# A hybrid decoder block in fp32: the S5 scan in eight blocks of four state columns on VectorE, and every gate, branch output, w_out and w_up chunk computed token-major

## The chip, the core and the metric

The kernel runs on one core of one Trainium2 chip. The metric is device time in microseconds (us) of one execution, the median of several runs. TensorE (PE) multiplies, VectorE (DVE), ScalarE (ACT) and GpSimd (POOL) do elementwise work, SyncE (SP) issues most of the loads. Each engine works through its own instructions in order. A "weight load" (PEld) is TensorE taking in the stationary operand of a matmul, which every matmul here does afresh.

## The reference

One decoder layer on 256 tokens of width 2048, all in float32:

```python
xn = rms_norm(h)
u_s5, u_lru, q, k, v, gate_logits = split(xn @ w_in)      # 1024 each, gates 3 x 2048
g_s5, g_lru, g_attn = split(sigmoid(gate_logits + b_gate))
merged = g_s5 * (s5(u_s5) @ w_br_s5) + g_lru * (rglru(u_lru) @ w_br_lru) + g_attn * (attn(q, k, v) @ w_br_attn)
h = h + merged @ w_out
h = h + relu(rms_norm(h) @ w_up) ** 2 @ w_down            # hidden width 8192
out = rms_norm(h)
```

S5: 64 groups of 16 channels with 64 complex states each. Per group, the input goes through a small matrix to the states (B), each state runs a linear recurrence h[t] = lam_bar * h[t-1] + bu[t] over the 256 tokens, the states go through another small matrix (C) to 16 outputs, and then come a skip term, tanh-GELU, and a gate through w_glu. RG-LRU is a gated real recurrence, attention is stick-breaking (exp, log and a running sum by a triangular product) in 8 heads.

## The kernel before

**Weight stream.** All large products draw on one stream of 520 weight units of 256 x 512 (512 KB). A unit is loaded on SP into `raw` (three buffers, loads three units ahead), cast on ScalarE into `hi` (L134: rounded to the reduced format fp32r), and VectorE forms the rest, `lo = raw - hi` (L135). `hi` and `lo` have three buffers each and are made two units ahead. Activations are split the same way, and each product is the sum of three: hi by hi, hi by lo, lo by hi.

**Two forms of a unit.** `chunk` (L183, tile `mm_...`) is channel-major: the weights are stationary and 256 tokens move, 24 matmuls of 256 columns a unit, and the result has channels on partitions. `chunk_tok` (L203, tile `mt_...`) is token-major: 128 tokens of the activation are stationary and 512 weight columns move, 12 matmuls of 512 columns, tokens on partitions. Here 148 units are channel-major and 372 token-major. A chunk is 512 output columns: 8 units where the input is 2048 wide, 4 where it is 1024.

**Order of work.** The stages follow one another in the stream: LRU input, S5 input, gates and branch product of LRU (branch 1), q, k and v with attention, gates and product of attention (branch 2), gates of S5, w_glu, product of S5, w_out, then four quarters of the MLP, each 32 units of w_up and 32 of w_down. What is not a weight unit is a side task: a generator in `later(..., rate)`. After each unit, `pump` gives each task as many steps as its rate (1.0 is a step a unit), and the instructions of a step are placed on their engines behind that unit's. `finish` runs a task to its end at once.

**S5.** `s5_scan` (L583) is such a task at rate 1.2. It runs in 16 blocks of NT = 2 state columns (a column holds 128 of the 4096 states). In a block, `s5_tables` makes cos and sin of the turning angle (`tc`, `ts`): the angle sum on POOL, rounding on ScalarE and VectorE (L557), magnitude and two sines on ScalarE (L559 to L561), which needs ScalarE's table for sine (ACT_TABLE_LOAD). Six small DMAs on SP put the operands of the B products side by side (`stk`, two buffers). The B products `ps_v` (L600) are copied to `v` (L602). Two products and a sum a component turn the states back by the angle (L614 to L620; L614, `t4 = vr * s`, on POOL), four scans (L628) run the recurrence with the real radius `rad`, each of 256 tokens, and six more products and sums turn forward (L630 to L638; L630 on POOL). Then eight matmuls of 32 output rows, L647 and L648, form `ps_y`: a block uses two of the array's four groups of 32 columns (`tile_position`). L650 adds the skip term to `us5`. After every fourth block GELU of a pair of column tiles runs on POOL, its tanh on ScalarE.

**Gates and branches.** `gates` (L685) and `branch` (L706) do three of four column chunks token-major and chunk 3 channel-major. The products are gated on VectorE and summed on POOL into `merged`; its token-major chunks are transposed by `blocks` (L673, 32 x 32 blocks on VectorE, L677) in `split_tok` while the next units run, and split into hi and lo.

**w_out and MLP.** w_out's chunks 0 to 2 are token-major; their residual sums are transposed in the side task `residual` and split. Chunk 3 is channel-major, and `to_tokens` transposes its sum the other way, sixteen blocks ahead of the sums of the second norm (`norm2`). In each MLP quarter, chunks 0 to 2 of w_up are token-major (`hidden`: transposes, square on ScalarE into `hd_hi` and on POOL, L991 the difference `hd_lo`), and chunk 3 is channel-major and needs no transpose (L1016). w_down is token-major.

Of the kernel before, what the change touches and what calls it, by code (L numbers as in the profile page):

```python
# [14 lines left out]
P = 128  # L15
L = 256
# [7 lines left out]
NT = 2  # L24
PAR = {"norm_mix_g": 16, "norm_mlp_g": 16, "b_gate": 48, "s5_d": 8, "s5_b_glu": 8, "lru_conv_b": 8,
# [12 lines left out]
GELU_C = math.sqrt(2.0 / math.pi)  # L38

# [6 lines left out]
def hybrid_block(ctx: ExitStack, tc: tile.TileContext, io, out):  # L46
# [213 lines left out]
    stk = sp.tile([96, 2, NT, 2, L], F32R, name="stk")  # L260
# [90 lines left out]
    cco = pp.tile([P, 2, 32, 16], F32, tag="v", name="cco")  # L351
# [13 lines left out]
    def s5_params():  # L365
# [55 lines left out]
        for k, (p, q, op) in enumerate(((cb_, ib_, ALU.add), (ib_, cb_, ALU.subtract))):  # L421
            u = [pp.tile([P, 32, 16], F32, tag=f"t{2 * k + i + 1}", name=f"cq{k}_{i}") for i in range(2)]
            g.tensor_tensor(u[0], cco[:, 0], p, ALU.mult)
            yield
            g.tensor_tensor(u[1], cco[:, 1], q, ALU.mult)
            yield
            for h in range(2):
                r_ = slice(64 * h, 64 * h + 64)
                g.tensor_tensor(ce[r_, k, :, h, :], u[0][r_], u[1][r_], op)
                yield  # L430
# [45 lines left out]
    def lru_half(c, us):  # L476
        parts = []
        for m in range(2):
            src = ((lp, "xc"), (lp, "r"), (lp, "i"), (lp, "th")) if m == 0 else ((pp, "tc"), (pp, "ts"), (pp, "t2"), (pp, "t4"))
            t = [p_.tile([P, 2, L], F32, tag=n_, name=f"lru_{n_}{c}", **({"bufs": 2} if n_ in ("tc", "ts") else {})) for p_, n_ in src]  # L480
# [62 lines left out]
    S5_RATE = 1.2  # L543

    def s5_tables(b):
# [7 lines left out]
        def gen():  # L553
            nc.gpsimd.tensor_tensor(c, fhi[:, q, :].unsqueeze(3).broadcast_to(sh), flo[:, q, :].unsqueeze(2).broadcast_to(sh), ALU.add)
# [19 lines left out]

    def s5_stack(b, ts=range(NT)):
        if b >= 32 // NT:
            return
        for t in ts:
            k = (b % 2) * NT + t
            for i, w_ in enumerate((ux[:, 0:4:2, :], ux[:, 1:3, :], ux[:, 0:4:3, :])):  # L580
                nc.sync.dma_start(stk[i * 32:i * 32 + 32, b % 2, t].bitcast(F32), w_[k * 32:k * 32 + 32].bitcast(F32))

    def s5_scan():  # L583
        tabs, more = s5_tables(0)
# [4 lines left out]
        s5_stack(0)  # L589
        for _ in range(5):  # L590
            yield
        for b in range(32 // NT):
            c, s = tabs
            ct = b // 2
            v = pp.tile([P, 2, NT, L], F32, tag="v", name=f"v{b}")
            vr, vi = v[:, 0], v[:, 1]
            for t in range(NT):
                ps = pss.tile([P, CH], F32, tag="ps", name=f"ps_v{b}")
                for i in range(2):
                    nc.tensor.matmul(ps[:, i * L:(i + 1) * L], stk[:, b % 2, t, 1, i * P:(i + 1) * P], stk[:, b % 2, t, 0, :], start=i == 0, stop=True,  # L600
                                     skip_group_check=True)
                nc.scalar.copy(v[:, :, t, :], v2(ps))  # L602
            if b % 2 and ct + 1 < WT:
                s5_split(ct + 1)
            more = iter(())
            if b + 1 < 32 // NT:
                tabs, more = s5_tables(b + 1)
            next(more, None)
            yield
            t1 = pp.tile([P, NT, L], F32, tag="t1", name=f"t1_{b}")  # L610
            t2 = pp.tile([P, NT, L], F32, tag="t2", name=f"t2_{b}")
            t3 = pp.tile([P, NT, L], F32, tag="t3", name=f"t3_{b}")
            t4 = pp.tile([P, NT, L], F32, tag="t4", name=f"t4_{b}")
            nc.gpsimd.tensor_tensor(t4, vr, s, ALU.mult)  # L614
            nc.vector.tensor_tensor(t1, vr, c, ALU.mult)
            nc.vector.tensor_tensor(t2, vi, s, ALU.mult)
            yield
            nc.vector.tensor_tensor(t1, t1, t2, ALU.add)
            nc.vector.tensor_tensor(t3, vi, c, ALU.mult)
# [19 lines left out]
            for _ in range(3):  # L639
                yield  # L640
# [466 lines left out]
```

## Time and profile before

| | |
|---|---|
| median of three runs | 1566.22 us (1565.44 to 1566.68) |
| the profiled execution, own time | 1565.52 us |
| its span in the profile | 1563.8 us |
| mean granted TensorE clock | 0.992 of full speed |
| TensorE busy | 1520.8 us, 97% |
| VectorE, ScalarE, POOL busy | 1162.6, 807.9, 219.0 us |
| S5's stretch (first LRU gate to w_glu) | 113.16 to 645.64 us |
| the MLP | from 847.46 us |

Rows of groups read: line, engine, operation, output <- inputs with shape, count | busy us, mean ns of one | idle time just before them and what ended it. Rows in order of time read: start and duration in us, engine, line, operation. Rows of waits read: waiting instruction <- what released it: us in all, count, longest.

### The profile page before, as it was taken

How to read it: one execution, taken by the hardware profiler on the slowest of the kernel's cores; microseconds unless marked ns; L12 is line 12 of the kernel's file. 1: busy time of each engine (PE TensorE's matmuls, PEld its weight loads, DVE VectorE, ACT ScalarE, POOL GpSimd, SP SyncE). 2: the span in 40 equal slices, each digit the busy share in tenths (PEclk: the TensorE clock that was granted, in tenths of full speed). 3: DMA queues.
4: the chain of work that ended last, by engine and by line, in shares of the span. 5: the costliest groups of instructions: out<-in, count | busy, mean ns of one | idle time of the engine just before them, and what ended most of it. 6: DMA issues, size and time to landing. Idle time of an engine off the chain costs nothing.

```text
span 1563.8 us, 21927 instructions
## 1 busy us (share of the span) xinstructions
PE 1520.8 (97%) x8430; PEld 1316.4 (84%) x8430; DVE 1162.6 (74%) x1417; ACT 807.9 (52%) x976; POOL 219.0 (14%) x172
## 2 busy tenths in 40 slices
PE   9899999989999999999999999999999999999997
PEld 9897789978877788988889888888988898888986
DVE  5887998878979899578698895558655685558755
ACT  7468555486756555543444544344433444344443
POOL 5301113112112322101000010000100000000111
PEclk9999999999999999999999999999999999999999
DMA  9555665545536565655756556555566566655554
GB/s 282 156 169 172 188 197 174 176 135 168 178 115 199 172 188 176 205 192 167 279 191 194 183 167 197 194 193 191 189 194 196 189 190 192 196 190 192 191 196 148
DMA packets 88491, 291.78 MB, mean 187 GB/s; under 512 B 12738, under 2 KB 16962, under 8 KB 88130
## 3 DMA queue, kind: packets, MB, share of 16 engines
q1 hardware_dynamic: 87954, 287.14, 57.2%
q10 hardware_dynamic: 432, 3.24, 0.6%
q8 instruction: 66, 1.08, 0.3%
q14 instruction: 39, 0.32, 0.1%
HBM read 281.95 MB, written 2.10 MB: 182 GB/s over the span
## 4 chain that ended last, share of the span: by engine, by line
PE 80%; DVE 11%; ACT 4%; issue 3%; DMA 1%; DVEq 0%; ACTq 0%
PE mt_w_down L212 7%; PE mt_w_down L213 7%; PE mt_w_down L214 7%; PE mm_w_in L198 5%; PE mm_w_in L196 5%; PE mt_w_up L214 5%; PE mm_w_in L197 5%; PE mt_w_up L213 5%; PE mt_w_up L212 5%; DVE lo L135 4%; PE mt_w_in L213 3%; PE mt_w_in L214 3%; PE mt_w_in L212 3%; PE mm_w_up L198 2%; PE mm_w_up L197 2%
## 5 line engine op out<-in xcount | busy, mean ns | idle before, releaser
L135 DVE TENSOR_TENSOR lo<-raw,hi 128x1024 fp32r<-128x1024 f32 (+1 forms) x521 | 660.9, 1272 | 327.6 <-ACT hi L134 323.0
L134 ACT CAST hi<-raw 128x1024 fp32r<-128x1024 f32 (+1 forms) x521 | 545.3, 1049 | 661.2 <-PE mt_w_down L214 197.6
L198 PE MATMUL mm_w_in<-xhi,lo 128*128 128x256 f32 x704 | 202.1, 288 | 7.3 <-DVE lo L135 7.3
L196 PE MATMUL mm_w_in<-xhi,hi 128*128 128x256 f32 x704 | 202.4, 288 | 1.8 <-DVE rs L297 1.2
L213 PE MATMUL mt_w_down<-lo,hd_hi 128*128 128x512 f32 (+1 forms) x528 | 202.1, 383 | 0.0
L212 PE MATMUL mt_w_down<-hi,hd_hi 128*128 128x512 f32 (+1 forms) x528 | 202.1, 383 | 0.0
L214 PE MATMUL mt_w_down<-hi,hd_lo 128*128 128x512 f32 (+1 forms) x528 | 202.0, 383 | 0.0
L197 PE MATMUL mm_w_in<-xlo,hi 128*128 128x256 f32 x704 | 201.3, 286 | 0.0
L213 PE MATMUL mt_w_up<-lo,hhi 128*128 128x512 f32 x384 | 150.0, 391 | 2.5 <-DVE lo L135 2.5
L214 PE MATMUL mt_w_up<-hi,hlo 128*128 128x512 f32 x384 | 149.5, 389 | 0.0
L212 PE MATMUL mt_w_up<-hi,hhi 128*128 128x512 f32 x384 | 149.4, 389 | 0.0
L213 PE MATMUL mt_w_in<-lo,xhi 128*128 128x512 f32 x352 | 140.8, 400 | 7.5 <-DVE lo L135 7.3
L212 PE MATMUL mt_w_in<-hi,xhi 128*128 128x512 f32 x352 | 141.4, 403 | 3.9 <-ACT hi L134 3.9
L198 PEld LDWEIGHTS mm_w_in<-xhi,lo 128*128 128x128 f32 x704 | 136.9, 195 | 9.5 <-DVE lo L135 9.1
L196 PEld LDWEIGHTS mm_w_in<-xhi,hi 128*128 128x128 f32 x704 | 137.3, 195 | 4.1 <-issue 2.6
L214 PE MATMUL mt_w_in<-hi,xlo 128*128 128x512 f32 x352 | 139.4, 396 | 0.0
L197 PEld LDWEIGHTS mm_w_in<-xlo,hi 128*128 128x128 f32 x704 | 137.3, 195 | 0.2
L214 PEld LDWEIGHTS mt_w_down<-hi,hd_lo 128*128 128x128 f32 x528 | 99.2, 188 | 19.4
L212 PEld LDWEIGHTS mt_w_down<-hi,hd_hi 128*128 128x128 f32 x528 | 99.2, 188 | 19.3
L213 PEld LDWEIGHTS mt_w_down<-lo,hd_hi 128*128 128x128 f32 x528 | 99.2, 188 | 19.2
L988 POOL TENSOR_TENSOR reluT<-reluT 128x1024 f32<-128x1024 f32 x12 | 23.8, 1984 | 642.9 <-ACT hd_hi L987 519.5
L213 PEld LDWEIGHTS mt_w_up<-lo,hhi 128*128 128x128 f32 x384 | 72.1, 188 | 19.3 <-DVE lo L135 4.5
(328 smaller groups left out, 2600.0 us busy)
## 6 DMA issues: line engine op xcount, KB each, us to landing
raw<-in_w_in SPq DMA_DIRECT2D x175, 512.0 KB, 3.6
raw<-in_w_up SPq DMA_DIRECT2D x128, 512.0 KB, 3.4
raw<-in_w_down SPq DMA_DIRECT2D x128, 512.0 KB, 4.1
raw<-in_w_out SPq DMA_DIRECT2D x32, 512.0 KB, 4.3
raw<-in_w_br_lru SPq DMA_DIRECT2D x16, 512.0 KB, 3.8
raw<-in_w_br_attn SPq DMA_DIRECT2D x16, 512.0 KB, 3.5
raw<-in_w_br_s SPq DMA_DIRECT2D x16, 512.0 KB, 3.5
stk<-ux SPq DMA_DIRECT2D x96, 64.0 KB, 3.3
```

The costliest lines, as they stand in the source:

```text
L134: anchor["act"] = nc.scalar.copy(h[:, k, :], r[:, k, :]).ins
L135: anchor["dve"] = nc.vector.tensor_tensor(l_[:, k, :], r[:, k, :], h[:, k, :].bitcast(F32), ALU.subtract).ins
L196: nc.tensor.matmul(o, wh[:, kk, s], xh, start=first and ct % 2 == 0, stop=False, skip_group_check=True)
L197: nc.tensor.matmul(o, wh[:, kk, s], xl, start=False, stop=False, skip_group_check=True)
L198: mm = nc.tensor.matmul(o, wl[:, kk, s], xh, start=False, stop=last and ct % 2 == 1, skip_group_check=True)
L212: nc.tensor.matmul(banks[j], xh[:, s], wh[:, a:b], start=kt == 0, stop=False)
L213: nc.tensor.matmul(banks[j], xh[:, s], wl[:, a:b], start=False, stop=False)
L214: return nc.tensor.matmul(banks[j], xl[:, s], wh[:, a:b], start=False, stop=kt == ng * UK - 1)
L988: nc.gpsimd.tensor_tensor(rT, rT, rT, ALU.mult)
```

## The change

1. NT goes from 2 to 4, so S5 has 8 blocks of four state columns, and elementwise operations in it work on 1024 elements a partition instead of 512. All of them are on VectorE, the table's angle sum and GELU's products too; scans run onto their own input. `stk` has one buffer, and its DMAs are issued in the scan steps, three behind each of the first four scans. The rate is 1.27, with about one large VectorE operation to a step. The C products of a block are 16 matmuls over all four column groups, neighbours in different groups. GELU becomes a side task of its own with two operations on ScalarE and two on VectorE, and its factor of one half moves into w_glu's split and gate.
2. `gates` and `branch` do all four chunks token-major, as do w_out and w_up in every quarter: 76 units change from 24 matmuls of 256 columns to 12 of 512. `split_tok(3)`, `residual(3)` and `hidden` of the last chunk now run as side tasks at rate 2.0 (two groups of four transposes a unit), and the units that need their result finish them first (`ms`, `hs`, `hs_`). `to_tokens` is gone.

```diff
-NT = 2
+NT = 4
-    stk = sp.tile([96, 2, NT, 2, L], F32R, name="stk")
+    stk = sp.tile([96, NT, 2, L], F32R, name="stk")
-    S5_RATE = 1.2
+    S5_RATE = 1.27
-            nc.gpsimd.tensor_tensor(c, fhi[...], flo[...], ALU.add)
+            nc.vector.tensor_tensor(c, fhi[...], flo[...], ALU.add)
     def s5_scan():
...
+            tt(t1, vr, c, ALU.mult)
+            yield
+            tt(t2, vi, s, ALU.mult)
+            yield
+            tt(t1, t1, t2, ALU.add)
+            yield
+            tt(t3, vi, c, ALU.mult)
+            yield
+            tt(vr, vr, s, ALU.mult)
+            yield
+            tt(t3, t3, vr, ALU.subtract)
             next(more, None)
             yield
...
+            for x_ in (t1, t3):
                 for t in range(NT):
                     j = b * NT + t
+                    tt_scan(x_[:, t, :], rad[:, j:j + 1].broadcast_to([P, L]), x_[:, t, :])
+                    if b + 1 < WT and x_ is t1:
+                        s5_stack(t)
+                    yield
...
+            for k, w_ in enumerate((t2, t1)):
+                for t in range(NT):
+                    nc.tensor.matmul(ps[t * 32:t * 32 + 32, 0:L], ce[:, k, b * NT + t, :, :], w_[:, t, :], start=k == 0, stop=k == 1,
+                                     skip_group_check=True, tile_position=(0, t * 32))
...
+    def gelu(b):
+        y = us5[:, b - 1:b + 1, :]
+        nc.scalar.activation(g1, y, AF.Square)
+        nc.vector.scalar_tensor_tensor(g1, g1, 1.0 / GELU_K, y, ALU.add, ALU.mult)
+        yield
+        nc.scalar.activation(g1, g1, AF.Tanh, scale=GELU_C * GELU_K)
+        nc.vector.scalar_tensor_tensor(y, g1, 1.0, y, ALU.add, ALU.mult)
...
-        banks = (chunk_tok if c < 3 else chunk)("w_in", GATE0 + 4 * idx + c, D, xs)
+        banks = chunk_tok("w_in", GATE0 + 4 * idx + c, D, xs)
-        banks = (chunk_tok if c < 3 else chunk)(wname, c, W, ys)
+        banks = chunk_tok(wname, c, W, ys)
+    last = later([split_tok(3, mlp.tile([P, 4, L], F32, tag="reluT", name="mT3", bufs=2))], 2.0)
-        rq = later([residual(c)], 1.0)
-    banks = chunk("w_out", 3, D, ms)
+        rq = later([residual(c)], 2.0 if c == 3 else 1.0)
     def norm2():
-        yield from to_tokens()
+        while rq[0]:
+            yield
-            banks = (chunk if last else chunk_tok)("w_up", ...)
+            banks = chunk_tok("w_up", ...)
+            hq = later([hidden(r, h_[:, k, :], l_[:, k, :], f"{q}_{c}")], 2.0 if c == FQ // CH - 1 else 1.0)
         def hs_(kt):
+            if kt >= 12:
+                finish(hq)
```

How it moves instructions, at three places. A row is a line, an operation, output <- inputs with the tiles' running numbers, and the shape; lines are those of the kernel the list is of.

VectorE in a block of S5, from one `lo` of the weight stream to the next in the kernel before (`us_99` is `us5`, `t_3` are t1 to t4):

```order
L135 TENSOR_TENSOR lo_2286<-raw_2247,hi_2285 128x1024
L615 TENSOR_TENSOR t_3_2301<-v_2265,tc_2055 128x512
L616 TENSOR_TENSOR t_3_2302<-v_2265,ts_2056 128x512
L619 TENSOR_TENSOR t_3_2303<-v_2265,tc_2055 128x512
L618 TENSOR_TENSOR t_3_2301<-t_3_2301,t_3_2302 128x512
L620 TENSOR_TENSOR t_3_2303<-t_3_2303,t_3_2304 128x512
L557 SCALAR_TENSOR_TENSOR ts_2281<-ts_2281,tc_2280 128x512
L715 TENSOR_TENSOR merged<-mt_w_br_lru_0_64_2203,gate_2_0_2197 128x512
L715 TENSOR_TENSOR merged<-mt_w_br_lru_1_64_2204,gate_2_1_2200 128x512
L135 TENSOR_TENSOR lo_2323<-raw_2283,hi_2322 128x1024
```

The same place in the changed kernel, a whole backward turn (`s_v` is v, `s_t` holds t1 and t2, `t_2` is t3, L558 is the angle sum of the next table, L136 makes `lo`):

```order
L136 TENSOR_TENSOR lo_2552<-raw_2510,hi_2551 128x1024
L615 TENSOR_TENSOR s_t<-s_v,tc_2094 128x1024
L617 TENSOR_TENSOR s_t<-s_v,ts_2095 128x1024
L136 TENSOR_TENSOR lo_2584<-raw_2549,hi_2583 128x1024
L619 TENSOR_TENSOR s_t<-s_t 128x1024
L136 TENSOR_TENSOR lo_2615<-raw_2581,hi_2614 128x1024
L621 TENSOR_TENSOR t_2_2472<-s_v,tc_2094 128x1024
L136 TENSOR_TENSOR lo_2646<-raw_2612,hi_2645 128x1024
L623 TENSOR_TENSOR s_v<-s_v,ts_2095 128x1024
L558 TENSOR_TENSOR tc_2534<-fhi,flo 128x1024
L625 TENSOR_TENSOR t_2_2472<-t_2_2472,s_v 128x1024
L136 TENSOR_TENSOR lo_2679<-raw_2643,hi_2678 128x1024
```

Eight operations of 512 elements stood between two `lo`; now at most three of 1024 stand there, and the turn is spread over five units. L623, before on POOL, is among them.

ScalarE in the first attention of the kernel before (L752 to L755 are a head's logits, their magnitude, exp and log; L559 to L561 the sines of a table):

```order
L752 COPY z_3391<-ps_z_3393 128x384
L559 ACTIVATE tc_3298<-ts_3299 128x512
L753 ACTIVATE s_3392<-z_3391 128x384
L560 ACT_TABLE_LOAD
L560 ACTIVATE ts_3299<-ts_3299 128x512
L754 ACT_TABLE_LOAD
L754 ACTIVATE s_3392<-s_3392 128x384
L561 ACT_TABLE_LOAD
L561 ACTIVATE tc_3298<-tc_3298,half_pi 128x512
L755 ACT_TABLE_LOAD
L755 ACTIVATE s_3392<-s_3392 128x384
```

ScalarE at the same place of the changed kernel (L743 to L746 are the head, L572 and L576 the split of the next block's operands, L607 copies B products):

```order
L761 ACT_TABLE_LOAD
L135 CAST hi_3153<-raw_3114 128x1024
L607 COPY s_v<-ps_v_3132 128x2x256
L607 COPY s_v<-ps_v_3136 128x2x256
L743 COPY z_3140<-ps_z_3142 128x384
L572 CAST ux<-us_99 128x256
L744 ACTIVATE s_3141<-z_3140 128x384
L576 ACTIVATE ux<-bco,par 128x2x64
L745 ACTIVATE s_3141<-s_3141 128x384
L576 ACTIVATE ux<-bco,par 128x2x64
L746 ACTIVATE s_3141<-s_3141 128x384
```

A head and a table's sines no longer alternate, and one table load stands ahead of the head instead of four in it. Over the whole program the list has 50 table loads before and 31 after.

VectorE from the last transposes of a quarter's third w_up chunk on, before (L991 and L1016 make `hd_lo`, L1016 that of the last chunk):

```order
L677 STREAM_TRANSPOSE reluT_2_8653<-relu_2_8618 32x2x4x32 x4
L135 TENSOR_TENSOR lo_8763<-raw_8726,hi_8762 128x1024
L135 TENSOR_TENSOR lo_8795<-raw_8760,hi_8794 128x1024
L135 TENSOR_TENSOR lo_8825<-raw_8792,hi_8824 128x1024
L991 TENSOR_TENSOR hd_lo_2_8617<-reluT_2_8653,hd_hi_2_8616 128x1024
L135 TENSOR_TENSOR lo_8856<-raw_8822,hi_8855 128x1024
L1016 TENSOR_TENSOR hd_lo_2_8617<-relu_3_0_8883,hd_hi_2_8616 128x512
L135 TENSOR_TENSOR lo_8898<-raw_8853,hi_8897 128x1024
L1016 TENSOR_TENSOR hd_lo_2_8617<-relu_3_1_8888,hd_hi_2_8616 128x512
L135 TENSOR_TENSOR lo_8916<-raw_8895,hi_8915 128x1024
```

And from the third chunk's `hd_lo` (L974) on in the changed kernel:

```order
L974 TENSOR_TENSOR hd_lo_2_7844<-reluT_2_7868,hd_hi_2_7843 128x1024
L136 TENSOR_TENSOR lo_7999<-raw_7977,hi_7998 128x1024
L136 TENSOR_TENSOR lo_8022<-raw_7996,hi_8021 128x1024
L683 STREAM_TRANSPOSE reluT_3_8037<-relu_3_8014 32x2x4x32 x8
L136 TENSOR_TENSOR lo_8049<-raw_8019,hi_8048 128x1024
L683 STREAM_TRANSPOSE reluT_3_8037<-relu_3_8014 32x2x4x32 x8
L136 TENSOR_TENSOR lo_8075<-raw_8046,hi_8074 128x1024
L136 TENSOR_TENSOR lo_8095<-raw_8072,hi_8094 128x1024
L974 TENSOR_TENSOR hd_lo_2_7844<-reluT_3_8037,hd_hi_2_7843 128x1024
L136 TENSOR_TENSOR lo_8114<-raw_8092,hi_8113 128x1024
```

Two subtractions of 512 became sixteen transposes in two runs of eight and one subtraction of 1024, each run between two `lo` of the first units of w_down.

236 lines of the change are left out of this document (87 added, 149 removed).

## The prediction

> **What bounds the kernel now.** I read the page first (busy times, chain), then the stages as windows, then who waited for whom in the stage that holds S5, then single groups and a few rows in order of time.
>
> ```profile
> PE 1520.8 (97%) x8430; PEld 1316.4 (84%) x8430; DVE 1162.6 (74%) x1417; ACT 807.9 (52%) x976; POOL 219.0 (14%) x172
> PE 80%; DVE 11%; ACT 4%; issue 3%; DMA 1%; DVEq 0%; ACTq 0%
> ```
>
> TensorE is the bound almost everywhere, and DMA is not (1% of the chain). But a busy matmul row hides waits, because ends are modelled. So I look at start-to-start distances by stage:
>
> ```profile
> core 0: us, PE busy (x) PEld busy (x) DVE busy (x) ACT busy (x) POOL busy (x), PEclk, DMA share, GB/s
> 113.16:645.64 532.48, 509.29 (x2914) 433.33 (x2913) 453.73 (x543) 328.96 (x426) 118.97 (x75) 0.98 0.55 174
> 645.64:847.46 201.82, 201.07 (x1201) 179.82 (x1200) 158.62 (x214) 92.93 (x109) 14.16 (x8) 1.00 0.62 205
> 847.46:918.31 70.85, 67.44 (x295) 54.05 (x294) 61.43 (x86) 36.52 (x41) 4.87 (x2) 1.00 0.55 176
> 1028.39:1093.67 65.28, 65.28 (x289) 54.05 (x288) 48.09 (x60) 29.85 (x31) 3.79 (x2) 1.00 0.58 188
> 1093.67:1116.70 23.03, 23.03 (x193) 23.03 (x192) 18.84 (x26) 10.46 (x12) 1.89 (x1) 1.00 0.61 200
> ```
>
> The last two rows are the yardstick: 24 token-major units of w_up took 65.28 us (2.720 a unit; 288 matmuls of 512 columns, 0.2267 us apart), and 8 channel-major units 23.03 us (2.879 a unit; 192 matmuls of 256 columns, 0.1199 us apart). Neither has a gap. The first window row is S5's stretch, from the first LRU gate to w_glu: 160 units (48 of gates and branch 1, 48 of q, k, v, 48 of gates and branch 2, 16 of S5 gates), of which 56 are channel-major. That is 104 x 2.720 + 56 x 2.879 = 444 us, of 532.5. The other 88 us are side matmuls and waits. The waits of weight loads there:
>
> ```profile
> PEld mt_w_in L213 <- DVE lo L135: 11.4, 9, 3.3
> PEld mt_w_in L212 <- ACT hi L134: 5.0, 3, 3.3
> PEld mm_w_in L198 <- DVE lo L135: 4.8, 5, 2.1
> PEld ps_y L647 <- issue: 4.0, 11, 0.7
> PEld ps_c L763 <- issue: 4.0, 2, 2.5
> PEld mt_w_br_lru L213 <- DVE lo L135: 2.9, 2, 1.6
> PEld ps_c L763 <- ACT v L602: 2.3, 1, 2.3
> ```
>
> With the 15 smaller rows these come to 44 us. Some 2 of them are the C products' change-over, priced below, and 42 are waits: TensorE waits for VectorE's `lo` (19), for ScalarE's `hi`, and for what attention owes its own products. VectorE is busy 453.7 us there, 92% of the 490 us without the waits. So this stretch is bound by TensorE with VectorE right behind it, and bursts on VectorE and ScalarE come through.
>
> **The change, part by part.** *Token-major everywhere.* 76 units go from 24 matmuls of 256 to 12 of 512: the fourth column chunk of three gates (24) and three branches (12), of w_out (8), and of w_up in each quarter (32). 76 x (2.879 - 2.720) = 12.1 us off, on TensorE, which has no gap in those rows. The Trainium skill (TensorE: Matmul & The Clock Gate, Back-to-back issue gap) gives N/2.4 + 2.5 ns, so 24 x 109.2 against 12 x 215.8, which an estimate by that page makes 0.03 us a unit and 2.4 us in all; the trace's 119.9 and 226.7 are larger by 11 each, a cost per matmul that halving the count halves, so I go by the rows.
>
> *C products.* Before, each block's 8 matmuls run in two column groups:
>
> ```profile
> 198.08 0.63 PE L647 MATMUL ps_y<-t,ce 128*32 128x256 f32 x4
> 198.54 0.61 PE L648 MATMUL ps_y<-t,ce 128*32 128x256 f32 x4
> 199.08 0.39 PE L600 MATMUL ps_v<-stk 96*128 96x256 f32 x1
> ```
>
> That is 1.00 us from the first to what follows: four pairs, 0.21 apart, and 0.15 of change-over, 16 times. After, 16 matmuls in four groups, ordered so that neighbours differ in group. If four run at once, a block takes the same 1.00, eight times: 8.0 us off. If only two can, 8 x (8 x 0.21 + 0.15) = 14.6 us, 1.4 off. The pair already shares the array without slowing, so I take 8.0. The Trainium skill (same page, Part 3: Packing small matmuls — row/col tiling) has three column tiles at 2.38 times one; at that loss four quads would take 0.27 each, an estimate that leaves 6.2. No row here shows more than two at once.
>
> *S5's work on VectorE.* Prices from the stretch:
>
> ```profile
> L135 DVE TENSOR_TENSOR lo<-raw,hi 128x1024 fp32r<-128x1024 f32 x160 | 202.1, 1271 | 44.1 <-ACT hi L134 43.6
> L628 DVE TENSOR_TENSOR_SCAN t<-rad,t 128x256 f32<-128x256 f32 x64 | 54.7, 898 | 0.0
> L615 DVE TENSOR_TENSOR t<-v,tc 128x512 f32<-128x512 f32 x16 | 27.4, 1714 | 0.0
> L638 DVE TENSOR_TENSOR t<-t,v 128x512 f32<-128x512 f32 x16 | 20.6, 1288 | 0.9
> L618 DVE TENSOR_TENSOR t<-t,t 128x512 f32<-128x512 f32 x16 | 10.9, 681 | 0.0
> 157.46 1.26 DVE L628 TENSOR_TENSOR_SCAN t<-rad,t 128x256 f32<-128x256 f32 x2
> 210.68 2.32 DVE L628 TENSOR_TENSOR_SCAN t<-rad,t 128x256 f32<-128x256 f32 x2
> 209.79 2.66 POOL L630 TENSOR_TENSOR v<-t,ts 128x512 f32<-128x512 f32 x1 [7.69 <-DVE t L628]
> 901.53 1.22 DVE L309 TENSOR_TENSOR hT<-hT 128x1024 f32<-128x1024 f32 x1
> L134 ACT CAST hi<-raw 128x1024 fp32r<-128x1024 f32 x160 | 166.8, 1049 | 178.8 <-PE mt_w_in L214 59.5 <-PE mm_w_in L197 40.6 <-DMA raw<-in_w_in 40.6
> ```
>
> The same operation takes 0.68 in L618 and 1.71 in L615, which runs beside POOL's L614; two scans take 1.26 alone and 2.32 beside POOL's L630. So POOL's three operations a block cost VectorE (1.714 - 0.681) x 16 + (1.288 - 0.681) x 16 + (0.898 - 0.63) x 64 = 43 us. That goes, and so does 0.05 on each `lo` (1.271 against 1.22): 8. What comes: the two products a block, 16 x 1.22 = 20; the angle sum of eight tables, 10; GELU's eight fused operations, 5. Eleven products, sums and table roundings of 512 a block become half as many of 1024: 8 x 11 x (2 x 0.681 - 1.22) = 12 less. Net 453.7 - 28 = 426 us, against 532.5 - 42 - 8.0 - 3.8 (24 of the 76 units) = 479 us of TensorE: 89%, from 92%. The steps are also finer: in the lists ahead of the diff, three products of 1.22 between two `lo` (3.7 us) where eight operations of 0.68 stood (5.4). And ScalarE:
>
> ```profile
> L560 ACT ACT_TABLE_LOAD x14 | 18.0, 1283 | 0.2
> L754 ACT ACT_TABLE_LOAD x4 | 5.1, 1283 | 0.1
> L755 ACT ACT_TABLE_LOAD x4 | 5.1, 1283 | 0.1
> 342.94 0.67 PE L763 MATMUL ps_c<-s,tri 128*128 128x256 f32 x2 [2.14 <-DVE s L757]
> ```
>
> The lists have 31 table loads instead of 50; in the first attention twelve, among which TensorE waits in the last row, become one. Against that, a table step on 1024 elements (magnitude, load, two sines) is one piece of some 4.4 us on ScalarE (3 x 1.05 by the cast of that size, and 1.28), half as often but longer than before. Of 42 us of waits I keep 18: 5 at the start, where LRU and S5's first table coincide unchanged, 7 for seven sine steps, 6 for the two attentions. So 24 off. The ends: all 42 off, or none; and 20 us longer, if each of the 96 products and sums takes L615's extra half instead of L618's pace (48 us more, 474 of 479).
>
> *Where DMAs and queues change.* The 96 stack transfers stay on SP, now three behind each of four scans, one buffer instead of two; the block's B products, their only readers, are done eight steps earlier. Nothing waits that did not. Gate biases add three transfers on SP; the last reader of their buffer is at least four units back. Both cost nothing, hidden beside weight loads with DMA busy 55%.
>
> *Start of w_up.* 24 units took 70.85, 5.6 over the yardstick. Sixteen transposes and the norm's sums met the first hidden chunk there. The sums now come behind the last residual. I take half, 2.8 off (0 to 5).
>
> *New handovers.* The last chunk of w_out's input, of w_up's input and of each hidden quarter is now transposed under way:
>
> ```profile
> L677 DVE STREAM_TRANSPOSE reluT<-relu 32x256 f32<-32x256 f32 x48 | 20.9, 436 | 0.8
> L991 DVE TENSOR_TENSOR hd_lo<-reluT,hd_hi 128x1024 fp32r<-128x1024 f32 x3 | 3.6, 1214 | 0.0
> L988 POOL TENSOR_TENSOR reluT<-reluT 128x1024 f32<-128x1024 f32 x12 | 23.8, 1984 | 642.9 <-ACT hd_hi L987 519.5
> L1005 ACT ACTIVATE relu<-mt_w_up 128x512 f32<-128x512 f32 x24 | 14.3, 598 | 11.6 <-PE mt_w_up L214 10.6
> ```
>
> Eight transposes (3.5 us) and a `lo` (1.22) are 4.7 us for a unit of 2.72, twice running: VectorE falls 4.0 us behind. A unit's `hi` starts when the unit three back ends, so its `lo` has 2 x 2.72 - 1.05 - 1.22 = 3.2 us to spare. 0.8 us shows, at four quarters; with w_out 4 us. It is needed at the seventh of w_down's units, 16.3 us in: 1.2 + 7.0 + 1.05 + 1.98 + 1.21 = 12.4 for the chain itself. Ends: nothing, and 10.
>
> **Sum**, against the profiled execution's own 1565.5 (span 1563.8): 12.1 + 8.0 + 24 + 2.8 - 4 = 42.9, so 1522.6. The median of the runs is 0.7 above the profiled one: 1523. Three runs lie within 1.24 us, 0.08%, so 0.2% (3.1 us) is what can be told from no change.
>
> **Rivals.** *The waits stay.* VectorE is still at 89% by work, and ScalarE's sine steps are longer; then 24 goes back and the time is 1547. For it: the load by work alone hardly moved. Against: much of the wait is bursts, and those shrink. 0.17. *Only two C products at once:* 6.6 back, 1530. Against it stand the pairs at 0.21. 0.08. *The handovers cost double* because the `lo` lag and POOL's square add up: 2 us more at each of four, 1531. Against it: the window 645.64:847.46 holds a burst of eight transposes and 72 units, 44 x 2.720 + 28 x 2.879 = 200.3 of its 201.8 us. 0.04. *The gap per matmul is 2.5 ns:* halving the count saves 2.4, so 9.7 back, 1533; 119.9 ns in 192 matmuls speaks against it. 0.02. That is the Trainium skill's rule from above. *Slower: VectorE becomes the bound in S5's stretch.* All of S5 now runs there, in place, in forms that the trace does not have (scan onto its own input, angle sum with two repeated operands). To be slower by 3 us it must eat 46 us more than forecast: work beyond 479 us, so from 426 + 53 on just to bind, and about 100 us over forecast to lose, half a microsecond on each of some 200 new instructions. 0.05. *Nearly no waits left,* 8 or less: 1512. 0.02.
>
> **The numbers.** The forecast has 0.62, its own range 1513 to 1535. Faster by over 0.2% are all cases but the slower one and a tail of the first rival, where waits grow by some 20: 0.93, 0.02, 0.05. The range that holds eight in ten reaches from waits nearly gone (1508) to waits unchanged (1547).
>
> **What would show it.** Of the changed kernel's profile: w_up's quarters at 87.0 us of 32 units with no channel-major row (12.1); C products sixteen at a time in about 1 us, in starts of four (8.0); scans at 0.63 to 0.66 throughout, products at 1.22 and POOL with little but the merges (43 and 27); weight loads waiting under 20 us in S5's stretch, which should be near 497 us. Wrong it would be if VectorE's work there is above 460 us, if attention's products still wait, or if w_down's first chunk in each quarter is over 21.8 us by more than one.

## The result and the profile after

The changed kernel takes 1528.92 us (median of four runs, 1528.90 to 1530.02), 0.9768 of the time before, 95% interval 0.9756 to 0.978. The forecast was 1523 in a range of 1508 to 1547. The profiled execution took 1528.90 us, its span is 1527.0.

The first part of the page of the kernel after, and its chain of waits:

```profile
PE 1491.6 (98%) x7518; PEld 1261.0 (83%) x7518; DVE 1170.1 (77%) x1428; ACT 780.2 (51%) x918; POOL 113.2 (7%) x100
PE 83%; DVE 9%; ACT 3%; issue 3%; DMA 2%; SPq 0%; DVEq 0%; ACTq 0%
```

VectorE's share of the chain fell by two points only: TensorE still waits for it, in shorter pieces. The stages as windows: S5's stretch, from w_glu to w_out's end, the first quarter's w_up and w_down, and the second quarter's w_up.

```profile
core 0: us, PE busy (x) PEld busy (x) DVE busy (x) ACT busy (x) POOL busy (x), PEclk, DMA share, GB/s
113.47:610.01 496.54, 487.02 (x2626) 411.57 (x2625) 428.57 (x477) 301.40 (x374) 14.12 (x8) 0.99 0.61 187
610.01:813.09 203.08, 199.37 (x961) 166.66 (x960) 166.53 (x231) 92.89 (x108) 14.15 (x8) 1.00 0.64 203
813.09:901.77 88.68, 87.76 (x389) 72.39 (x388) 79.56 (x114) 47.09 (x52) 5.69 (x3) 1.00 0.62 189
901.77:990.52 88.75, 87.35 (x385) 72.02 (x384) 51.22 (x56) 35.29 (x35) 2.91 (x1) 1.00 0.62 194
990.52:1077.56 87.04, 87.04 (x385) 72.10 (x384) 66.75 (x85) 40.33 (x42) 5.69 (x3) 1.00 0.60 190
```

S5's stretch went from 532.48 to 496.54 us: 35.9 of the 36.8 us by which the span is shorter. w_glu to w_out went from 201.82 to 203.08, the first w_up (both of its old windows) from 93.86 to 88.68, w_down from 87.07 to 88.75, a later w_up from 88.31 to 87.04. The rows of the first w_up and w_down before:

```profile
847.46:941.32 93.86, 90.45 (x486) 77.06 (x485) 80.76 (x114) 46.95 (x52) 6.77 (x3) 1.00 0.55 180
941.32:1028.39 87.07, 87.07 (x386) 72.08 (x385) 44.58 (x41) 35.38 (x36) 2.89 (x2) 1.00 0.60 193
```

What weight loads waited for in S5's stretch, after:

```profile
PEld mt_w_in L214 <- DVE lo L136: 5.6, 8, 1.9
PEld mt_w_in L213 <- ACT hi L135: 3.8, 2, 3.1
PEld ps_y L653 <- issue: 3.0, 9, 0.4
PEld ps_v L605 <- issue: 2.9, 7, 0.4
PEld mt_w_br_attn L213 <- ACT hi L135: 2.6, 1, 2.6
```

VectorE's `lo` headed this list before with 11.4, 4.8 and 2.9, 19.1 in all; here it has 5.6, and 7.0 with two smaller rows. ScalarE's `hi` did not fall: 5.6 in all before, 7.7 here, so it is now waited for a little more than `lo`. Attention's `ps_c` is gone from the list. Groups of VectorE there:

```profile
L136 DVE TENSOR_TENSOR lo<-raw,hi 128x1024 fp32r<-128x1024 f32 x160 | 198.7, 1243 | 52.1 <-ACT hi L135 51.9
L660 DVE TENSOR_TENSOR_SCAN t<-rad,t 128x256 f32<-128x256 f32 x32 | 22.4, 712 | 0.0
L660 DVE TENSOR_TENSOR_SCAN s_t<-rad,s_t 128x256 f32<-128x256 f32 x32 | 21.4, 677 | 0.0
L621 DVE TENSOR_TENSOR t<-s_v,tc 128x1024 f32<-128x1024 f32 x8 | 10.8, 1354 | 0.0
L615 DVE TENSOR_TENSOR s_t<-s_v,tc 128x1024 f32<-128x1024 f32 x8 | 9.7, 1218 | 0.0
```

Scans take 0.69 us instead of 0.90, a little over the forecast's 0.63 to 0.66, and most products of 1024 take 1.22 (L621 1.35). And the C products, in order of time:

```profile
310.38 0.39 PE L215 MATMUL mt_w_in<-hi,xlo 128*128 128x512 f32 x1
310.70 1.07 PE L653 MATMUL ps_y<-s_t,ce 128*32 128x256 f32 x16
311.70 0.39 PE L605 MATMUL ps_v<-stk 96*128 96x256 f32 x1
```

Sixteen matmuls are followed 1.00 us later by the next product, where eight took that before.

By starts of consecutive products I split each stretch into products at their yardstick (226.7 and 119.9 ns), side matmuls, and the rest, which I call waits. A wait right behind a side matmul counts to the side matmuls. In S5's stretch that is 444.1 + 46.1 + 42.3 us before and 440.3 + 37.1 + 19.1 after.

### The profile page after: what moved, and what is told of

It reads as the page before. It is cut to its first block, busy times and chain, and to the rows that moved or that the text cites. A ratio compares the mean times of both kernels' runs of the same rounds, so it can differ in the third digit from the quotient of the medians.

```text
span 1527.0 us, 19937 instructions
## 1 busy us (share of the span) xinstructions
PE 1491.6 (98%) x7518; PEld 1261.0 (83%) x7518; DVE 1170.1 (77%) x1428; ACT 780.2 (51%) x918; POOL 113.2 (7%) x100
## 4 chain that ended last, share of the span: by engine, by line
PE 83%; DVE 9%; ACT 3%; issue 3%; DMA 2%; SPq 0%; DVEq 0%; ACTq 0%
PE mt_w_up L215 7%; PE mt_w_up L214 7%; PE mt_w_up L213 7%; PE mt_w_down L214 7%; PE mt_w_down L215 7%; PE mt_w_down L213 7%; PE mt_w_in L214 5%; PE mt_w_in L215 5%; PE mt_w_in L213 5%; PE mm_w_in L198 4%; PE mm_w_in L199 4%; PE mm_w_in L197 4%; DVE lo L136 4%; ACT hi L135 2%; DVE reluT L683 1%
## 5 line engine op out<-in xcount | busy, mean ns | idle before, releaser
L136 DVE TENSOR_TENSOR lo<-raw,hi 128x1024 fp32r<-128x1024 f32 (+1 forms) x521 | 657.2, 1265 | 305.9 <-ACT hi L135 297.1
L213 PE MATMUL mt_w_down<-hi,hd_hi 128*128 128x512 f32 (+1 forms) x528 | 202.1, 383 | 0.0
L215 PE MATMUL mt_w_down<-hi,hd_lo 128*128 128x512 f32 (+1 forms) x528 | 202.0, 383 | 0.0
L214 PE MATMUL mt_w_up<-lo,hhi 128*128 128x512 f32 x512 | 199.3, 389 | 0.0
L215 PE MATMUL mt_w_up<-hi,hlo 128*128 128x512 f32 x512 | 199.2, 389 | 0.0
L213 PE MATMUL mt_w_up<-hi,hhi 128*128 128x512 f32 x512 | 199.2, 389 | 0.0
L213 PE MATMUL mt_w_in<-hi,xhi 128*128 128x512 f32 x448 | 177.3, 397 | 2.9 <-ACT hi L135 2.9
L215 PE MATMUL mt_w_in<-hi,xlo 128*128 128x512 f32 x448 | 175.3, 391 | 0.0
L199 PE MATMUL mm_w_in<-xhi,lo 128*128 128x256 f32 x512 | 145.8, 286 | 3.1 <-DVE lo L136 3.0
L197 PE MATMUL mm_w_in<-xhi,hi 128*128 128x256 f32 x512 | 146.3, 286 | 1.7 <-DVE rs L298 0.9
L198 PE MATMUL mm_w_in<-xlo,hi 128*128 128x256 f32 x512 | 145.8, 285 | 0.0
L213 PEld LDWEIGHTS mt_w_down<-hi,hd_hi 128*128 128x128 f32 x528 | 99.2, 188 | 19.5
L215 PEld LDWEIGHTS mt_w_down<-hi,hd_lo 128*128 128x128 f32 x528 | 99.2, 188 | 19.3
L683 DVE STREAM_TRANSPOSE reluT<-relu 32x256 f32<-32x256 f32 x256 | 111.5, 436 | 4.1
L213 PEld LDWEIGHTS mt_w_up<-hi,hhi 128*128 128x128 f32 x512 | 96.1, 188 | 19.9
L215 PEld LDWEIGHTS mt_w_up<-hi,hlo 128*128 128x128 f32 x512 | 96.1, 188 | 19.9
L214 PEld LDWEIGHTS mt_w_in<-lo,xhi 128*128 128x128 f32 x448 | 84.6, 189 | 25.0 <-DVE lo L136 8.6
```

The source lines that it names most:

```text
L136: anchor["dve"] = nc.vector.tensor_tensor(l_[:, k, :], r[:, k, :], h[:, k, :].bitcast(F32), ALU.subtract).ins
L197: nc.tensor.matmul(o, wh[:, kk, s], xh, start=first and ct % 2 == 0, stop=False, skip_group_check=True)
L198: nc.tensor.matmul(o, wh[:, kk, s], xl, start=False, stop=False, skip_group_check=True)
L199: mm = nc.tensor.matmul(o, wl[:, kk, s], xh, start=False, stop=last and ct % 2 == 1, skip_group_check=True)
L213: nc.tensor.matmul(banks[j], xh[:, s], wh[:, a:b], start=kt == 0, stop=False)
L214: nc.tensor.matmul(banks[j], xh[:, s], wl[:, a:b], start=False, stop=False)
```

## The experiments

Each kernel was timed beside the kernel before on its own chip (medians 1564.3 to 1565.3 there). "Waits" are those of S5's stretch, split in this way; spans of stages are from the profile.

**Which part brings it.** First each half alone. `s5_only` has the changed S5 with the old gates, branches, w_out and w_up:

```diff
-        banks = chunk_tok("w_in", GATE0 + 4 * idx + c, D, xs)
+        banks = (chunk_tok if c < 3 else chunk)("w_in", GATE0 + 4 * idx + c, D, xs)
...
-            banks = chunk_tok("w_up", q * (FQ // CH) + c, D, hs)
+            banks = (chunk if last else chunk_tok)("w_up", ...)
```

> The changed kernel with its second part undone: gates and branches of chunk 3, w_out's and w_up's last chunk channel-major again, S5 as changed. Theory A (from the two traces): the S5 part is nearly the whole gain, since outside S5's stretch the shorter units give back what they save in late `lo` after the new transposes (8.3 us saved, 11 us of new waits, and 3.9 us won at w_up's start): 1565.8 - 32 = 1534 us, between 1531 and 1537. Rival B: the token-major units are worth their 12.1 us less small handovers, and S5's part is worth correspondingly less: 1539 to 1542 us.

1532.69 us (1529.99 to 1534.33), ratio 0.9798 (0.9781 to 0.9815). S5's stretch 498.5, waits 17.5. Theory A: S5 is nearly all of it. `tok_only` is the other half, the old S5 with every chunk token-major:

> The kernel before with the second part alone: all chunks token-major, S5 as before in 16 blocks with POOL. Theory A: 3.8 us off in S5's stretch and about 1 outside it, so 1561 us, between 1558 and 1564. Rival B: 12.1 + 2.8 - 4 = 11 us off, 1555 us.

1569.21 us (1566.51 to 1571.44), ratio 1.0027 (1.0017 to 1.0037): slower than before, which neither theory had. S5's stretch came as expected (529.4, 3.1 off), and so did w_up (88.67 and 87.04). But the first three w_down took 91.25, 89.05 and 91.15, and the last stage of the kernel, with the fourth, 100.20 instead of 96.33. TensorE's rows in the first of them, where the first column is the start:

```profile
943.90 0.39 PE L212 MATMUL mt_w_down<-hi,hd_hi 128*128 128x512 f32 x1
946.16 0.71 PE L213 MATMUL mt_w_down<-lo,hd_hi 128*128 128x512 f32 x1 [1.86 <-DVE lo L135]
946.66 0.63 PE L214 MATMUL mt_w_down<-hi,hd_lo 128*128 128x512 f32 x1
947.09 0.63 PE L212 MATMUL mt_w_down<-hi,hd_hi 128*128 128x512 f32 x1
949.64 0.42 PE L212 MATMUL mt_w_down<-hi,hd_hi 128*128 128x512 f32 x1
949.91 0.40 PE L213 MATMUL mt_w_down<-lo,hd_hi 128*128 128x512 f32 x1
```

The handover's wait is 2.03 us here and not 1.57 as in the changed kernel, and behind it seven products start 0.427 us apart until 949.6, at half speed, which costs 1.4 us more. In the quarter with 89.05 the wait was 1.87 and no slow spell came. The longer wait goes with the `hi` ahead of the transposes: here it had to wait 0.2 to 0.8 us for its weights to land in each of the four quarters, and in the changed kernel in none.

**POOL's contention.** `before_dve` moves POOL's three operations a block to VectorE in the kernel before:

```diff
-            nc.gpsimd.tensor_tensor(c, fhi[...], flo[...], ALU.add)
+            nc.vector.tensor_tensor(c, fhi[...], flo[...], ALU.add)
-            nc.gpsimd.tensor_tensor(t4, vr, s, ALU.mult)
+            nc.vector.tensor_tensor(t4, vr, s, ALU.mult)
-            nc.gpsimd.tensor_tensor(vr, t2, s, ALU.mult)
+            nc.vector.tensor_tensor(vr, t2, s, ALU.mult)
```

> The kernel before with the angle sum and the two products that were on POOL moved to VectorE, still 16 blocks, same steps. It tells POOL's contention from the size of steps. Contention theory: scans back to 0.63 to 0.66 us, products of L615 and L638's kind at 0.68; VectorE's busy time in S5's stretch falls by 43 + 8 - 33 = 18 us from 453.7 to about 436, and the waits fall from 42 to 25 or 30: 1549 to 1554 us. Step theory: what counts are operations between two `lo`, and these become ten of 0.68 instead of eight, so the waits stay at 40 or grow: 1563 to 1572 us.

1557.05 us (1554.64 to 1557.28), ratio 0.9947 (0.9932 to 0.9962). Its window of S5's stretch, and two groups:

```profile
114.36:635.45 521.09, 503.39 (x2914) 430.88 (x2913) 439.36 (x591) 329.05 (x426) 39.05 (x28) 0.99 0.55 177
L628 DVE TENSOR_TENSOR_SCAN t<-rad,t 128x256 f32<-128x256 f32 x64 | 40.1, 672 | 0.0
L614 DVE TENSOR_TENSOR t<-v,ts 128x512 f32<-128x512 f32 x16 | 13.1, 820 | 0.0
```

With 48 operations more (x591 for x543), VectorE was busy 439.4 us instead of 453.7, and waits fell from 42.3 to 30.6. Steps got longer, so the step theory is out for this part; the contention theory had the work right (436) and the time 3 us and more too low. Those 3 us are not in S5's stretch, which is 11.4 us shorter: in the profiled execution it begins 1.2 us later, and the first w_up takes 95.42 us instead of 93.86, with a spell of half clock at 906.6. `pool_back` does the reverse in the changed kernel:

```diff
-            nc.vector.tensor_tensor(c, fhi[...], flo[...], ALU.add)
+            nc.gpsimd.tensor_tensor(c, fhi[...], flo[...], ALU.add)
-            tt(vr, vr, s, ALU.mult)
+            nc.gpsimd.tensor_tensor(vr, vr, s, ALU.mult)
-            tt(vr, t3, s, ALU.mult)
+            nc.gpsimd.tensor_tensor(vr, t3, s, ALU.mult)
```

> The changed kernel with the angle sum and two of the products (vr * s backward, t3 * s forward) on POOL again, 24 operations of 1024. VectorE has 24 x 1.22 = 29 us less to do. Contention theory: in the kernel before each POOL operation of 512 cost VectorE 43 / 48 = 0.9 us, so here 24 x 1.8 = 43 us come on, scans and products beside POOL go to twice their time, and the subtraction that waits for POOL holds `lo` behind it in VectorE's queue: VectorE at about 443 us in S5's stretch, waits from 19 to 30 or 40, 1537 to 1550 us. Rival, that only the number and length of VectorE's own operations count: 1520 to 1529 us.

1548.63 us (1546.89 to 1550.13), ratio 0.9889 (0.987 to 0.9908):

```profile
114.32:628.53 514.21, 492.02 (x2626) 411.67 (x2625) 442.10 (x454) 301.22 (x374) 83.48 (x31) 0.99 0.58 181
L645 DVE TENSOR_TENSOR s_t<-s_t,ts 128x1024 f32<-128x1024 f32 x8 | 16.7, 2088 | 0.0
L636 DVE TENSOR_TENSOR s_t<-s_t,tc 128x1024 f32<-128x1024 f32 x8 | 14.1, 1768 | 0.0
```

VectorE has 23 operations less and 13.5 us more to do; products of 1.22 take 1.77 and 2.09 beside POOL. Waits rose from 19.1 to 33.1, about as foreseen.

**Step size.** `coarse` puts S5's products in threes and its scans in fours, with empty steps between them, in as many steps as before:

```diff
             tt(t1, vr, c, ALU.mult)
-            yield
             tt(t2, vi, s, ALU.mult)
-            yield
             tt(t1, t1, t2, ALU.add)
             yield
+            yield
+            yield
```

> The changed kernel with S5's operations in bursts: three products of 1024 a step, then empty steps, four scans a step, in the same number of steps. VectorE's work is the same. Contention theory: nothing but bursts changes, and a burst of 4 x 1.22 = 4.9 us is over the 3.2 us that a `lo` has to spare only at some blocks: 1529 to 1533 us. Step theory: the waits in S5's stretch go from 19 back to about 40: 1548 to 1552 us. If each of the 32 bursts costs 4.9 + 1.22 - 2.72 - 3.2 = 0.2 us, 6 us: 1535.

1533.51 us (1530.84 to 1535.02), ratio 0.9798 (0.9782 to 0.9814). S5's stretch 500.2, waits 22.9. Fine steps are worth 3.7 us, not 20.

**Where the sines fall.** `phase` delays one table of the changed kernel by eight empty steps and raises the rate behind it, so that S5 ends at the same place:

```diff
+            if b == 2:
+                for _ in range(8):
+                    yield
+                sq[1] = 1.38
             next(more, None)
             tt(t2, t1, c, ALU.mult)
```

> The changed kernel with eight empty steps in S5's third block ahead of the sines of its next table, and rate 1.38 from there on so that S5 ends at the same place. The only aim is to put the sines of one table among the four heads of the first attention on ScalarE, as they were in the kernel before (twelve table loads there instead of one). Coincidence theory: a good part of the 23 us of waits that went (about 9 of them at 334 to 357 us before) went because the sines of the changed kernel happen to miss both attentions; then attention's products wait again, 6 to 10 us more with the half clock after long waits: 1535 to 1540 us. Rival, that finer steps and VectorE alone did it: 1528 to 1531 us.

1548.09 us (1547.58 to 1550.73), ratio 0.9889 (0.9872 to 0.9907), 19 us more and twice what I expected. ScalarE in the first attention:

```profile
318.52 1.28 ACT L564 ACT_TABLE_LOAD   x1
319.81 1.06 ACT L564 ACTIVATE ts<-ts 128x1024 f32<-128x1024 f32 x1
320.89 1.28 ACT L749 ACT_TABLE_LOAD   x1
322.19 0.52 ACT L749 ACTIVATE s<-s 128x384 f32<-128x384 f32 x1
322.73 1.28 ACT L565 ACT_TABLE_LOAD   x1
...
340.50 1.28 ACT L749 ACT_TABLE_LOAD   x1
341.79 0.52 ACT L749 ACTIVATE s<-s 128x384 f32<-128x384 f32 x1
342.33 1.28 ACT L750 ACT_TABLE_LOAD   x1
```

The two sines (L564, L565) alternate with the head's exp and log (L749, L750), and exp and log then go on loading a table each, head by head. The trace has 47 table loads instead of 31 (50 before), since the shift put such a spell into the second attention too, there behind GELU's tanh (L672). Waits 34.4, nearly all of the difference between 320 and 350 and at 424 to 435 us.

So is the coincidence what the change removed? `before_hold` keeps the sines out of the heads in the kernel before, at a higher rate:

```diff
-    S5_RATE = 1.2
+    S5_RATE = 1.26
+            while busy[0]:        # ahead of the step with the sines
+                yield
+        busy[0] = True            # attention, ahead of its heads; False behind them
```

> The kernel before, with S5's sine steps held while the heads of an attention are on ScalarE, and S5's rate 1.26 instead of 1.2 so that it ends at the same place. VectorE's and POOL's work is unchanged, POOL's contention too. Coincidence theory: the waits at 334 to 357 us (9 us) and part of those at 445 to 449 (up to 6, half clock included) go, 9 to 14 us off: 1551 to 1556 us. Rival, that these waits come from VectorE and only change their place: 1561 to 1567 us.

1565.26 us (1563.37 to 1567.41), ratio 1.0003 (0.9994 to 1.0012): nothing, with 36 table loads instead of 50. Attention's `ps_c` waits no more, but `lo` is waited for as long as before (19.7 us), and C products wait 8.7 us for their operand (1.5 before): waits 32.7, side matmuls 54.3 instead of 46.1. The rival was right for this kernel. `dve_hold` has both edits:

> The kernel before with both single edits: the angle sum and the two products on VectorE instead of POOL, and the sine steps held during the heads of an attention (rate 1.26). Apart they gave 11.4 us and 1.4 us in S5's stretch (521.1 and 531.1 of 532.5). Theory of interplay: with POOL's contention gone VectorE has room for S5 at the higher rate, and then the 13 us of attention waits left at 329 to 351 and 440 to 443 us go too: stretch 508 to 513 us, 1545 to 1549 us in all, which with 9.4 us of C products and 3.8 of shorter units is what the whole change gives there. Additive theory: 519.7 us, 1555 to 1557 us. If holding costs by denser steps what it gains: 1557 us or more.

1550.08 us (1549.40 to 1551.09), ratio 0.9911 (0.9894 to 0.9927). S5's stretch 515.6 (16.8 off, against 11.4 + 1.4 apart), waits 22.8. More than the sum, less than I expected: removing the coincidence pays once VectorE has room.

**C products.** `c_order` issues them column by column:

```diff
-            for k, w_ in enumerate((t2, t1)):
-                for t in range(NT):
+            for t in range(NT):
+                for k, w_ in enumerate((t2, t1)):
```

> The changed kernel with the C products issued column by column (both products of state column 0, then both of 1, 2, 3), so neighbours are in the same column group. If the four groups start their matmuls independently of program order, as the pairs of the kernel before did (issued in this order and started 13 ns apart): still 1.00 us a block in starts of four, time unchanged within 1 us of the changed kernel's (1529). If matmuls start in program order: a block's 16 take 13 starts of 0.22 + 0.15 = 3.0 us, 2 more in each of eight blocks: 1545 us.

1531.23 us (1530.27 to 1531.90), ratio 0.9776 (0.9757 to 0.9795): 2 us over the changed kernel and so over what I expected, but the intervals of the two ratios overlap. In six of eight blocks the starts are in fours at 0, 240, 456 and 672 ns and the next product at 1.02 us, as in the changed kernel within 20 ns; the two others waited for an operand. The groups start on their own, ahead of program order.

**The handovers.** `spread` takes each new handover's first step at once and the others at rate 1.25:

```diff
-            hq = later([hidden(...)], 2.0 if c == FQ // CH - 1 else 1.0)
+            hq = later([hidden(...)], 1.25 if c == FQ // CH - 1 else 1.0)
+            if c == FQ // CH - 1:
+                step(hq)
```

> The changed kernel with the three new handovers spread: the first step is taken at once and the rate is 1.25 instead of 2.0, so four transposes stand between two `lo` where eight stood. Burst theory (1.22 + 3.57 us twice against 2.72 a unit, 4.6 us late against 3.2 to spare, 1.57 us of wait in each quarter): 1.77 + 1.22 = 3.0 a unit, about 1 us late after four, nothing shows; 4 x 1.6 = 6.3 us off in w_down and up to 1 in w_out: 1522 us, 1520 to 1524. Rival, that the chain to `hd_lo` (square, POOL's square, subtraction) then comes too late for the seventh unit: a wait of 1 us moves there in each quarter, 1525 to 1529 us.

1532.55 us (1530.38 to 1534.40), ratio 0.9786 (0.9768 to 0.9805): not faster. w_down did gain, 87.65 instead of 88.75, with 0.47 left where `hd_lo` is late (the rival's place, at half its price). But w_out lost 5.9 us (96.23) and the first w_up 2.0 (90.65). The wait in w_out:

```profile
PEld mt_w_out L213 <- ACT hi L135: 5.5, 2, 4.6
747.68 1.04 ACT L135 CAST hi<-raw 128x1024 fp32r<-128x1024 f32 x1 [4.30 <-DMA raw<-in_w_out]
748.77 1.22 PE L213 MATMUL mt_w_out<-hi,mg_yhi 128*128 128x512 f32 x2 [4.15 <-ACT hi L135]
749.79 1.05 PE L215 MATMUL mt_w_out<-hi,mg_ylo 128*128 128x512 f32 x2
```

The large wait is not VectorE's. Counted through, the two L213 rows at 748.77 belong to the ninth unit of w_out, the first of its second chunk, and the L215 rows behind them to the seventh: with the spread handover, two matmuls come ahead of their turn, and TensorE waits 4.3 us for a `hi` that it would need two units later. A spell of half clock behind it costs 2.3 us more. That `hi` in turn waits for its weights, whose load took 7.1 us from issue to landing (740.49 to 747.58; the median of w_out's loads is 4.2), while the residual input (2 MB, issued at 728.85) and the last gain (1 MB, at 738.18) come in. In the changed kernel the same load took 6.6 us, but the units keep their order there, and 0.7 us shows. `xres` was to part these transfers:

```diff
-    nc.scalar.dma_start(x_tok, io["x_res"])
     for c in range(4):
+        nc.scalar.dma_start(x_tok[:, :, s], io["x_res"][:, :, s])
...
     for q in range(NQ):
+        nc.scalar.dma_start(gfb[:, s], repeat(io["final_norm_g"][:, s], P))
```

> The changed kernel with the residual input x (2 MB, in one transfer at w_out's start) loaded in four pieces of 512 KB, each at the start of the w_out chunk that needs it, and the last norm's gain (1 MB, twelve units later) in four pieces in the MLP's quarters. DMA theory: w_out's waits at 734, 738 and 747 us (2.8 us) come from weights that land late behind these 3 MB while VectorE is already late by the new transposes: w_out 90.4 to 87.5 us, 1526 us in all. Rival, that the sixteen transposes alone make these waits: 1528 to 1529 us.

1528.36 us (1527.62 to 1528.75), ratio 0.9765 (0.9751 to 0.9778), w_out 89.63 instead of 90.37. It does not settle the question: nothing ties these issues to their chunk, and the trace shows x's four pieces issued between 726.97 and 736.41 and the gain's from 738.44 on, as close together as before. What w_out's 3 us would be with the transfers really apart stays open.

**A faster version.** `best` is the changed kernel with xres's edit, only `hidden` spread (rate 1.34), and branch 2's sums on VectorE:

> The changed kernel with three edits: only the hidden chunk's handover spread (first step at once, rate 1.34), x and the last gain loaded in pieces, and branch 2's sums into merged on VectorE instead of POOL. From the single runs: w_down 88.74 to 87.1 a quarter (6.4 us off in four), w_out 2.8 off, and the wait at 463 us, where a `lo` and a subtraction took 2.08 and 2.32 us beside POOL's sum, 1.6 off: 1528.9 - 10.8 = 1518 us, between 1516 and 1522. If a moved wait takes its place at the seventh unit of w_down (0.5 us a quarter as in the run with all handovers spread) 1520.

1521.27 us (1520.29 to 1525.02), ratio 0.9723 (0.9706 to 0.974), faster than both kernels and within the range that I expected, near the 1520 that I gave for a wait left at `hd_lo`. S5's stretch, w_out and the first w_down:

```profile
113.99:608.76 494.77, 487.29 (x2627) 412.78 (x2625) 426.22 (x485) 301.42 (x374) 0.00 (x0) 0.99 0.61 188
721.40:810.80 89.40, 87.63 (x385) 71.92 (x384) 79.64 (x119) 40.17 (x46) 3.54 (x2) 1.00 0.69 223
899.60:987.25 87.65, 87.35 (x385) 71.99 (x384) 52.23 (x56) 35.28 (x35) 1.90 (x1) 1.00 0.62 196
PEld mt_w_down L215 <- DVE hd_lo L973: 0.7, 1, 0.7
```

POOL has nothing left in S5's stretch, which is 1.8 us shorter; w_down gains 1.1 a quarter, and the same 0.47 at `hd_lo` stays.

## Why the prediction was right, and where not

- **Token-major units, 12.1 us:** right. A quarter's w_up, with eight of the units, fell from 88.31 to 87.04 us, 1.27 as 8 x 0.159. The rule of 2.5 ns between matmuls (the Trainium skill, TensorE: Matmul & The Clock Gate, Back-to-back issue gap) would have made that 0.25 us by the prediction's estimate; the trace disagrees. That section of the Trainium skill gives the rule for a matmul by itself, and about 131 ns at 512 columns for a stream of weight loads and matmuls, which these rows with 226.7 ns do not show either.
- **C products, 8.0:** right; four groups at once, 1.00 us a block. Side matmuls fell by 9.0, since blocks that waited for an operand became rarer. No four-way loss shows.
- **VectorE's work, 426 us in the stretch:** 428.6. POOL's contention and its direction were shown twice: in `before_dve` 35 us of operations came to VectorE and its busy time fell by 14.4, so some 50 us of contention went; in `pool_back` 28 us of operations left and it rose by 13.5, so some 42 came. The prediction had 43.
- **Waits in S5's stretch, 42 to 18:** 42.3 to 19.1. The size was right, the reason only in part, and the size partly by luck: of the 18 to stay, the prediction put 5 at the start and 6 into the two attentions, and the trace has 7.1 up to 160 us, 2.1 in the attentions and 6.5 in branch 2 (440 to 500 us). Contention is worth 12 to 14 of the waits, fine steps 4, and the table loads of attention, which the prediction had as a consequence of the change (50 to 31), are where sines happen to fall: eight empty steps, with a higher rate behind them, bring 16 of the 19 loads back, and 15 us of waits. These are more than the 23.2 that went, so they overlap; `before_hold` suggests why, since in the kernel before one wait that goes uncovers another. `dve_hold`, with POOL's work and the sines taken out together, has 22.8, 19.5 less; with the 3.8 of `coarse` that is the whole 23.2, though the two numbers come from different kernels.
- **Start of w_up, 2.8:** 3.9 (5.1 to 1.2 us of waits).
- **New handovers, +4:** this is the step that failed. They cost 11 instead of 4: w_down 1.68 us in each of four quarters (6.7), and 4.4 from w_glu to w_out's end, 3.2 of it in w_out and 1.2 ahead of it, behind transposes of an earlier chunk that the kernel before has too. The prediction's own sign of being wrong came with it: w_down's first chunk over 21.8 us by more than one. VectorE in the first w_down, and ScalarE at its start:

```profile
901.29 1.28 ACT L986 ACTIVATE relu<-mt_w_up 128x512 f32<-128x512 f32 x2 [0.98 <-PE mt_w_up L215]
902.46 1.04 ACT L135 CAST hi<-raw 128x1024 fp32r<-128x1024 f32 x1
907.41 1.06 ACT L135 CAST hi<-raw 128x1024 fp32r<-128x1024 f32 x1 [1.02 <-PE mt_w_down L215]
904.68 3.57 DVE L683 STREAM_TRANSPOSE reluT<-relu 32x256 f32<-32x256 f32 x8
908.28 1.22 DVE L136 TENSOR_TENSOR lo<-raw,hi 128x1024 fp32r<-128x1024 f32 x1
909.54 3.59 DVE L683 STREAM_TRANSPOSE reluT<-relu 32x256 f32<-32x256 f32 x8
913.16 2.36 DVE L136 TENSOR_TENSOR lo<-raw,hi 128x1024 fp32r<-128x1024 f32 x2
```

The 3.2 us to spare were right, the 4.0 us of lateness were not: the `lo` that begins at 913.16 belongs to a `hi` that ended at 908.47 (begun at 907.41), 4.7 us late, 4.2 of it by the two runs of transposes and some 0.5 because the two relus on ScalarE push the `hi` at 902.46 and with it the first run. No run moves the relus, so this last part is read from the rows and not tested. 1.57 us shows where 0.8 was forecast. For w_out the prediction gave 0.8 as well: 1.7 us is again a `lo` behind eight transposes (at 733.8), and the prediction left out that 3 MB of other loads come in just there. The profiled execution is 6.3 us above the sum: 7.1 by handovers and the 1.2 ahead of w_out, 0.8 by waits in S5's stretch that stayed, 0.5 at the start and outside the span, less 2.1 that C products and w_up's start gained above forecast.

Of the rivals, none happened. "Handovers double" is the nearest: its 8 us are close to the 7 more that they cost, but it had 2 us more at each of four quarters, where 0.9 came and the rest in w_out, and its reason, POOL's square, is not the one: no product of w_down waits for `hd_lo` in the changed kernel.

## What to carry to other kernels

An operation that takes longer beside a busy neighbour is priced from the same operation with and without the neighbour, and the gain comes even where the work moved is more than what the neighbour did. Before a lower count of table loads or waits is credited to a change, shift the phase of the side work by a few steps: 15 us here hung on eight empty steps and the rate that made up for them. In the kernel before, 14 loads fewer brought nothing, so a count of loads is no price either. A handover is late by everything ahead of it on every engine, so the evacuation counts too. Spreading it paid 1.1 us a quarter in w_down and cost 5.9 in w_out, where matmuls then came ahead of their turn beside a large load: look at the order of TensorE's rows after such a change.

## What the runs showed of the hardware

- TensorE's clock falls to half after waits of about two microseconds. After the first 70 us and before the last 12, the fourteen traces have 40 spells of half granted clock, each of 3.41 us or twice that, in which products of 512 columns start 427 ns apart instead of 227. By starts of consecutive products, none of 47 single waits of 1.5 to 1.93 us has a spell within 6 us behind it, one of 1.95 does, and so do 33 of 41 waits of 2.0 us and more. The other seven spells follow two waits within 4 us, of 1.26 and 0.70 us in six traces and of 1.08 and 1.05 in one; behind the same pair the changed kernel has no spell. A page's rule stands behind it: the Trainium skill (TensorE: Matmul & The Clock Gate, Part 1: The HAM clock gate) has half the clock after at least one idle window of about 3.4 us. The 3.4 us agree with the length of the spells, but here waits well shorter than that were enough. In `tok_only` such a spell makes a wait of 2.03 us cost 3.4, in three of four quarters, and is how that kernel came out slower than the kernel before.
- Matmuls of different column groups start ahead of program order: sixteen issued column by column started in fours, 13 ns apart, as did those issued in turn (7 ns apart).
